# A gated short-convolution layer in split fp32: the products of each piece of weights in other orders

## The chip, the cores and the metric

One core of a Trainium2 chip runs the whole layer in one launch. The metric is device time in microseconds, as the median of several executions.

## The reference

With depth 1 the reference is one layer of 256 tokens and 2048 features, 4096 channels wide:

```python
h = rmsnorm(x, norm_g)
shift, scale, gate = split(silu(c) @ ada_w + ada_b, 3)
h = h * (1 + scale) + shift
b_gate, c_gate, v, g = split(h @ w_in, 4)      # w_in: 2048 x 16384
u = causal_depthwise_conv(c_gate * v, conv_w)  # width 3
y = (b_gate * u * silu(g)) @ w_out             # w_out: 4096 x 2048
x = x + gate * y
return rmsnorm(x, final_g)
```

Everything is float32. The two large products are with `w_in` (134 MB) and `w_out` (33.5 MB); `ada_w` (50 MB) is multiplied by a single vector.

## The kernel before

**Split numbers.** A float32 number is kept as two parts whose sum is the number: `hi`, the number rounded to what one pass of TensorE carries (type float32r), and `lo`, the rest. `split(raw, n)` (lines 187 to 193) makes them from a piece of weights: ACT casts `raw` to `hi` (L191), then DVE subtracts (L192). The tokens lie in `hT` as two such parts, `hh_` and `hl_` (256 columns each, one beside the other), and `y` likewise. A product of two split numbers takes three terms: hi by hi, hi by the tokens' lo, and the weights' lo by hi. The fourth, lo by lo, is left out.

**Start (`mm_s`).** While adaLN's shift and scale are still being summed up from `ada_w` (on DVE, lines L236 and L238), products are already taken for 16 of the 32 channel tiles: four chunks (`ch`) of four tiles (`CT`), each in its four quarters of `w_in`. `plan()` (L41) writes out by hand in which order pieces of `ada_w` are loaded and parts of products are taken. `part(ch, q, k0, k1)` takes the products of feature tiles k0 to k1 for one quarter of a chunk. It loads pieces of up to 2048 numbers per partition, splits them, and for each feature tile and each of the four channel tiles `m` issues three products of 256 columns, one behind another: L286 (hi by `hh_`), L291 (hi by `hl_`), L292 (lo by `hh_`). Two channel tiles share a PSUM bank; `acc` sums up the parts (ACT for the first, DVE L300 for the others). Where adaLN's sums of a group of features are complete, TensorE turns them (`tp_g`, L247), and the tokens of these features get their scale and shift.

**Middle (`mm_b`).** The other 16 channel tiles are taken two at a time, in eight rounds (`ct`), each over the four quarters, each quarter in two pieces of eight feature tiles. For each piece, the loop over `m` (two tiles, a bank each) stands outside and the loop over the feature tile `i` inside; each `i` issues one product of 512 columns (L382: hi by both parts of the tokens) and one of 256 columns (L385: lo by `hh_`). Beside that the gate's columns of `ada_w` are loaded and summed up (`gate_piece`, with its product `ps_gate`, L362).

**End (`mm_o`).** The product with `w_out` runs over four blocks of 512 output columns (`dc`). `out_mm` takes a piece of four channel tiles for one of the two tiles of tokens (`t`) with three products of 512 columns per channel tile: L426 (y hi by hi), L427 (y hi by lo), L428 (y lo by hi). In the last block the last three pieces of the second token tile are held back (`late`), so that the first token tile's norm runs beside them.

**What sets the order.** Every engine works through its own queue in order. All loads are issued by SP. A scheduler orders each queue when the program is built, by its own estimate of times; so the order in the source is where it starts from, not the order that runs. `raw`, `hi` and `lo` have three buffers each, the product banks six. Each product loads its weights anew: there are as many LDWEIGHTS as MATMUL instructions.

Of the kernel before, what the change touches and what calls it, by code (L numbers as in the profile page):

```python
# [13 lines left out]
P = 128  # L14
D = 2048
E = 4096
T = 256
KT = D // P
NCT = E // P
# [10 lines left out]
# In units of the load of one 128 x 128 block: how far adaLN's loads stay behind the products, what lies between the  # L30
# load of a feature tile's columns and its use, and the products of one block.
# [3 lines left out]
# Numbers per partition of a piece of w_in or w_out and of a piece of ada_w; slots of CT * T numbers.  # L35
# [53 lines left out]
def short_conv_layer(ctx: ExitStack, tc: tile.TileContext, x, c, norm_g, ada_w, ada_b, w_in, conv_w, w_out, final_g, out):  # L89
# [49 lines left out]
    # The square root's table is fetched before the squares' sum asks for it.  # L139
# [24 lines left out]
    # The tokens' transpose lies in xs until its features' scale and shift are known, then in hT as two parts that  # L164
    # sum to it.
# [21 lines left out]
    def split(raw, n):  # L187
        """raw = hi + lo, exactly, each of them a number that one pass carries."""
        hi = wpool.tile([P, SLOT], F32R, tag="hi", name="hi", bufs=3)
        lo = wpool.tile([P, SLOT], F32R, tag="lo", name="lo", bufs=3)  # L190
        nc.scalar.copy(hi[:, :n], raw[:, :n])  # L191
        nc.vector.tensor_tensor(out=lo[:, :n], in0=raw[:, :n], in1=hi[:, :n].bitcast(F32), op=ALU.subtract)  # L192
# [23 lines left out]
    def ada_piece(k0, nk, piece):  # L216
# [5 lines left out]
        # Two sums in turn where nothing else stands between them.  # L222
# [20 lines left out]
        # The sum over partitions: turned, then summed along the free axis.  # L243
# [20 lines left out]
    def part(ch, q, k0, k1):  # L264
        """The products of feature tiles k0 to k1 for one quarter of a chunk."""
        col = q * E + ch * CT * P
        step = SLOT // (CT * P)
        banks = [psum.tile([P, 512], F32, tag="mm", name="mm_s") for _ in range(CT // 2)]
        for s0 in range(k0, k1, step):
# [8 lines left out]
            for i in range(sk):  # L278
                k = s0 + i
                hh, hl = hh_[:, k], hl_[:, k]  # L280
                for m in range(CT):
                    o = slice((i * CT + m) * P, (i * CT + m + 1) * P)
                    dst = banks[m // 2][:, (m % 2) * T : (m % 2 + 1) * T]
                    # One start per bank: it clears the whole bank's flags, so the other half's first product lands.
                    opens = k == k0 and m % 2 == 0
                    first = nc.tensor.matmul(dst, hi[:, o], hh, start=opens, stop=False, skip_group_check=True)  # L286
                    if opens:
                        opener = first
                    elif k == k0:
                        tc.add_manual_dep(first.ins, opener.ins.name, after, reason="the bank's flags are cleared first")  # L290
                    nc.tensor.matmul(dst, hi[:, o], hl, start=False, stop=False, skip_group_check=True)  # L291
                    nc.tensor.matmul(dst, lo[:, o], hh, start=False, stop=k == k1 - 1, skip_group_check=True)  # L292
# [11 lines left out]
    def mixed(ch):  # L304
        """y of a chunk's channel tiles, whose four parts are in acc."""
# [61 lines left out]
    for ct in range(NS, NCT, 2):  # L367
        for q in QUARTERS:
            banks = [psum.tile([P, 2, T], F32, tag="mm", name="mm_b") for _ in range(2)]
            col = q * E + ct * P  # L370
            for kp in range(0, KT, KP):
# [6 lines left out]
                for m in range(2):  # L378
                    for i in range(KP):
                        k = kp + i  # L380
                        o = slice((i * 2 + m) * P, (i * 2 + m + 1) * P)
                        nc.tensor.matmul(  # L382
                            banks[m].rearrange("p a t -> p (a t)"), hi[:, o], hT[:, k, :], start=k == 0, stop=False, skip_group_check=True
                        )
                        nc.tensor.matmul(banks[m][:, 0, :], lo[:, o], hh_[:, k], start=False, stop=k == KT - 1, skip_group_check=True)  # L385
# [33 lines left out]
    def out_mm(po, t, ep, hi, lo):  # L419
        for i in range(EP):  # L420
            ct = ep * EP + i
            y = ys[ct // 2][:, ct % 2]
            yh = y[:, 0, t * P : (t + 1) * P]
            yl = y[:, 1, t * P : (t + 1) * P]
            o = slice(i * 512, (i + 1) * 512)
            nc.tensor.matmul(po, yh, hi[:, o], start=ct == 0, stop=False)  # L426
            nc.tensor.matmul(po, yh, lo[:, o], start=False, stop=False)  # L427
# [85 lines left out]
```

## Time and profile before

| | us |
|---|---|
| median of 3 runs | 954.27 |
| lowest, highest | 953.95, 955.4 |
| profiled execution: span from the first to the last instruction | 951.9 |

The profiled execution has no time of its own beside its span; the median lies 2.4 us above that span, and this is taken for what lies around it. Instruction starts are recorded; the ends of matmuls are modelled, so that a matmul is drawn longer than the distance to the next one. The distance between starts is what a product costs.

### The profile page before, as it was taken

To read this page: it belongs to the slowest core of one execution; us is meant where nothing else is said; L and a number is where in the kernel's file an instruction comes from. 1 tells how busy PE (TensorE), PEld (TensorE's weight loads), DVE (VectorE), ACT (ScalarE), POOL (GpSimd) and SP (SyncE) were. 2 spreads that over 40 slices of the span, in tenths; PEclk is the share of its full clock that TensorE was granted. 3 is DMA by queue.
4 is the path that set the end of the run, shared out by engine and by line. 5 is a ranking of instruction groups with operands and counts; after the bars stand their busy time and mean duration, and the time that the engine had idled before them with its cause. 6 is when DMAs were issued, how large, how long until landed. Compare 5 with 4: busy or idle time off the path is not lost.

```text
span 951.9 us, 14329 instructions
## 1 busy us (share of the span) xinstructions
PE 917.5 (96%) x5963; PEld 834.8 (88%) x5963; DVE 667.7 (70%) x785; ACT 418.2 (44%) x468; POOL 0.7 (0%) x6
## 2 busy tenths in 40 slices
PE   3699999999999999999999999999999999999996
PEld 2699999999999999988888888888888878888884
DVE  4798998899899998997565556556555654454533
ACT  6575342443435444444443544444444433433332
POOL 0000000000000000000000000000000000000000
PEclk9799999999999999999999999999999999999998
DMA  9999997999988887886655665565556585665532
GB/s 271 298 360 368 283 337 251 326 329 321 366 296 290 256 261 237 281 298 200 198 195 178 193 203 179 185 199 190 177 184 201 191 309 180 198 198 177 180 130 88
DMA packets 172048, 227.51 MB, mean 239 GB/s; under 512 B 5792, under 2 KB 112464, under 8 KB 171600
## 3 DMA queue, kind: packets, MB, share of 16 engines
q1 hardware_dynamic: 171984, 226.61, 73.0%
q8 instruction: 46, 0.75, 0.3%
q14 instruction: 18, 0.15, 0.0%
HBM read 224.49 MB, written 2.10 MB: 238 GB/s over the span
## 4 chain that ended last, share of the span: by engine, by line
PE 90%; DMA 4%; DVE 3%; issue 1%; ACT 1%; SPq 1%; ACTq 0%; DVEq 0%
PE mm_b L382 25%; PE mm_b L385 13%; PE mm_s L292 11%; PE mm_s L286 11%; PE mm_s L291 11%; PE mm_o L427 6%; PE mm_o L426 6%; PE mm_o L428 6%; DMA raw_s<-in_sc_w_in_dram 2%; DMA at<-in_ada_w_dram 2%; DVE lo L192 1%; DMA x<-in_x_dram 1%; DVE gv L238 1%; ACT hi L191 0%; SPq L231 0%
## 5 line engine op out<-in xcount | busy, mean ns | idle before, releaser
L382 PE MATMUL mm_b<-hT,hi 128*128 128x512 f32 x1024 | 355.2, 392 | 0.0
L286 PE MATMUL mm_s<-hT,hi 128*128 128x256 f32 x1024 | 286.9, 284 | 9.2 <-ACT hT L261 4.9
L291 PE MATMUL mm_s<-hT,hi 128*128 128x256 f32 x1024 | 287.2, 283 | 0.0
L385 PE MATMUL mm_b<-hT,lo 128*128 128x256 f32 x1024 | 285.4, 280 | 0.0
L292 PE MATMUL mm_s<-hT,lo 128*128 128x256 f32 x1024 | 282.9, 283 | 1.4 <-DVE lo L192 1.3
L192 DVE TENSOR_TENSOR lo<-raw,hi 128x2048 fp32r<-128x2048 f32 x64 | 146.6, 2291 | 128.4 <-ACT hi L191 128.3
L382 PEld LDWEIGHTS mm_b<-hT,hi 128*128 128x128 f32 x1024 | 192.1, 188 | 42.3 <-issue 0.2
L191 ACT CAST hi<-raw_s 128x2048 fp32r<-128x2048 f32 (+3 forms) x85 | 126.5, 1489 | 177.5 <-PE mm_s L291 120.7
L286 PEld LDWEIGHTS mm_s<-hT,hi 128*128 128x128 f32 x1024 | 194.3, 191 | 10.2 <-ACT hT L261 5.1
L291 PEld LDWEIGHTS mm_s<-hT,hi 128*128 128x128 f32 x1024 | 195.1, 191 | 0.2 <-issue 0.2
L292 PEld LDWEIGHTS mm_s<-hT,lo 128*128 128x128 f32 x1024 | 191.9, 190 | 2.3 <-DVE lo L192 2.1
L385 PEld LDWEIGHTS mm_b<-hT,lo 128*128 128x128 f32 x1024 | 192.3, 188 | 0.5 <-issue 0.2
L191 ACT CAST hi<-raw 128x2048 fp32r<-128x2048 f32 x64 | 122.4, 1912 | 158.0 <-PE mm_b L382 103.1
L192 DVE TENSOR_TENSOR lo<-raw_s,hi 128x2048 fp32r<-128x2048 f32 (+3 forms) x85 | 149.5, 1759 | 19.7 <-ACT hi L191 19.2
L192 DVE TENSOR_TENSOR lo<-raw_o,hi 128x2048 fp32r<-128x2048 f32 x32 | 73.4, 2292 | 85.4 <-ACT hi L191 85.4
L191 ACT CAST hi<-raw_o 128x2048 fp32r<-128x2048 f32 x32 | 61.2, 1913 | 105.1 <-PE mm_o L428 92.3
L427 PE MATMUL mm_o<-lo,y 128*128 128x512 f32 x256 | 101.8, 399 | 0.0
L426 PE MATMUL mm_o<-hi,y 128*128 128x512 f32 x256 | 101.0, 396 | 0.0
L428 PE MATMUL mm_o<-hi,y 128*128 128x512 f32 x256 | 100.1, 392 | 0.0
L238 DVE SCALAR_TENSOR_TENSOR gv<-at,silu_c,gv 128x512 f32<-128x512 f32 (+1 forms) x149 | 92.2, 639 | 2.6 <-DMA at<-in_ada_w_dram 1.9
L426 PEld LDWEIGHTS mm_o<-hi,y 128*128 128x128 f32 x256 | 48.1, 188 | 12.6 <-issue 0.2
L428 PEld LDWEIGHTS mm_o<-hi,y 128*128 128x128 f32 x256 | 48.1, 188 | 11.5
(80 smaller groups left out, 441.8 us busy)
## 6 DMA issues: line engine op xcount, KB each, us to landing
raw<-in_sc_w_in_dram SPq DMA_DIRECT2D x64, 1024.0 KB, 5.6
raw_s<-in_sc_w_in_dram SPq DMA_DIRECT2D x46, 1024.0 KB, 7.5
at<-in_ada_w_dram SPq DMA_DIRECT2D x128, 256.0 KB, 6.6
raw_o<-in_sc_w_out_dram SPq DMA_DIRECT2D x32, 1024.0 KB, 5.1
at_g<-in_ada_w_dram SPq DMA_DIRECT2D x32, 512.0 KB, 6.8
raw_s<-in_sc_w_in_dram SPq DMA_DIRECT2D x19, 512.0 KB, 5.8
raw_s<-in_sc_w_in_dram SPq DMA_DIRECT2D x7, 768.0 KB, 7.6
raw_s<-in_sc_w_in_dram SPq DMA_DIRECT2D x13, 256.0 KB, 4.5
```

What stands on the lines that cost most here:

```text
L191: nc.scalar.copy(hi[:, :n], raw[:, :n])
L192: nc.vector.tensor_tensor(out=lo[:, :n], in0=raw[:, :n], in1=hi[:, :n].bitcast(F32), op=ALU.subtract)
L238: nc.vector.scalar_tensor_tensor(out=g2, in0=at4[:, i], scalar=c_k, in1=g2, op0=ALU.mult, op1=ALU.add)
L286: first = nc.tensor.matmul(dst, hi[:, o], hh, start=opens, stop=False, skip_group_check=True)
L291: nc.tensor.matmul(dst, hi[:, o], hl, start=False, stop=False, skip_group_check=True)
L292: nc.tensor.matmul(dst, lo[:, o], hh, start=False, stop=k == k1 - 1, skip_group_check=True)
L382: nc.tensor.matmul(banks[m].rearrange("p a t -> p (a t)"), hi[:, o], hT[:, k, :], start=k == 0, stop=False, skip_group_check=True)
L385: nc.tensor.matmul(banks[m][:, 0, :], lo[:, o], hh_[:, k], start=False, stop=k == KT - 1, skip_group_check=True)
L426: nc.tensor.matmul(po, yh, hi[:, o], start=ct == 0, stop=False)
L427: nc.tensor.matmul(po, yh, lo[:, o], start=False, stop=False)
L428: nc.tensor.matmul(po, yl, hi[:, o], start=False, stop=ct == NCT - 1)
```

## The change

The three terms of each piece are issued in other orders. Nothing is added or removed: each product has the same operands and the same bank. In the start the order depends on the chunk, in the middle on the round, at the end on the block. Where a bank's first product must come first, the flag for it and the dependency follow the new order. Comments are dropped too, which moves line numbers only.

```diff
+BIG_ORDERS = [
+    lambda kp: [(i, m, j) for m in range(2) for i in range(kp) for j in range(2)],
+    lambda kp: [(i, m, j) for i in range(kp) for j in range(2) for m in range(2)],
+    lambda kp: [(i, m, j) for m in range(2) for j in range(2) for i in range(kp)],
+    lambda kp: [(i, m, j) for j in range(2) for i in range(kp) for m in range(2)],
+]
+MM_ORDERS = [
+    [(m, j) for m in range(CT) for j in range(3)],
+    [(m, j) for j in range(3) for m in range(CT)],
+    [(m, j) for h in range(2) for j in range(3) for m in (h, h + 2)],
+    [(m, j) for j in range(3) for m in (0, 2, 1, 3)],
+]
...
     def part(ch, q, k0, k1):
...
-            for i in range(sk):
+            terms = [(i, m, j) for i in range(sk) for m, j in MM_ORDERS[ch]]
+            for i, m, j in terms:
                 k = s0 + i
-                hh, hl = hh_[:, k], hl_[:, k]
-                for m in range(CT):
-                    o = slice((i * CT + m) * P, (i * CT + m + 1) * P)
-                    dst = banks[m // 2][:, (m % 2) * T : (m % 2 + 1) * T]
...
-                    first = nc.tensor.matmul(dst, hi[:, o], hh, start=opens, stop=False, skip_group_check=True)
...
-                    nc.tensor.matmul(dst, hi[:, o], hl, start=False, stop=False, skip_group_check=True)
-                    nc.tensor.matmul(dst, lo[:, o], hh, start=False, stop=k == k1 - 1, skip_group_check=True)
+                o = slice((i * CT + m) * P, (i * CT + m + 1) * P)
+                dst = banks[m // 2][:, (m % 2) * T : (m % 2 + 1) * T]
...
+                ins = nc.tensor.matmul(
+                    dst, (lo if j == 2 else hi)[:, o], (hl_ if j == 1 else hh_)[:, k], start=opens, stop=j == 2 and k == k1 - 1, skip_group_check=True
+                )
...
                 hi, lo = split(raw, SLOT)
-                for m in range(2):
-                    for i in range(KP):
-                        k = kp + i
-                        o = slice((i * 2 + m) * P, (i * 2 + m + 1) * P)
+                for i, m, j in BIG_ORDERS[(ct - NS) // 2 % 4](KP):
+                    k = kp + i
+                    o = slice((i * 2 + m) * P, (i * 2 + m + 1) * P)
+                    if j == 0:
                         nc.tensor.matmul(
                             banks[m].rearrange("p a t -> p (a t)"), hi[:, o], hT[:, k, :], start=k == 0, stop=False, skip_group_check=True
                         )
+                    else:
                         nc.tensor.matmul(banks[m][:, 0, :], lo[:, o], hh_[:, k], start=False, stop=k == KT - 1, skip_group_check=True)
...
-    def out_mm(po, t, ep, hi, lo):
+    def out_mm(po, ts, ep, hi, lo, order):
         for i in range(EP):
...
+            if order == 0:
+                terms = [(t, j) for t in ts for j in range(3)]
+            elif order == 1:
+                terms = [(t, j) for j in range(3) for t in ts]
+            else:
+                terms = [(t, j) for t in ts for j in (0, 2, 1)]
...
-            out_mm(po[0], 0, ep, hi, lo)
-            if dc == 3 and ep >= n_ep - LATE:
-                late.append((ep, hi, lo))
-            else:
-                out_mm(po[1], 1, ep, hi, lo)
+            if dc == 3:
+                out_mm(po, [0], ep, hi, lo, 0)
+                if ep >= n_ep - LATE:
+                    late.append((ep, hi, lo))
+                else:
+                    out_mm(po, [1], ep, hi, lo, 0)
+            else:
+                out_mm(po, [0, 1], ep, hi, lo, dc)
```

The first entry of each list is the order of before, so chunk 0, the rounds 0 and 4 of the middle and block 3 of the end keep theirs. In block 0 only the loop over the two token tiles moves inside the loop over the channel tiles.

More of the change, by code (lines that the diff above doesn't have):

```diff
@@ L277, in part @@
             hi, lo = split(raw, n)
[L278 removed]
+            terms = [(i, m, j) for i in range(sk) for m, j in MM_ORDERS[ch]]
+            for i, m, j in terms:
                 k = s0 + i
[L280 to L292 removed]
+                o = slice((i * CT + m) * P, (i * CT + m + 1) * P)
+                dst = banks[m // 2][:, (m % 2) * T : (m % 2 + 1) * T]
+                opens = k == k0 and m % 2 == 0 and j == 0
+                ins = nc.tensor.matmul(
+                    dst, (lo if j == 2 else hi)[:, o], (hl_ if j == 1 else hh_)[:, k], start=opens, stop=j == 2 and k == k1 - 1, skip_group_check=True
+                )
+                if opens:
+                    openers[m // 2] = ins
+                elif k == k0 and j == 0:
+                    tc.add_manual_dep(ins.ins, openers[m // 2].ins.name, after, reason="the bank's flags are cleared first")
         if k0 == 0:
```

13 lines of the change are left out of this document (7 added, 6 removed).

## The prediction

> **What bounds the kernel now.** I read the page's head first, then the table of waits of TensorE, then a table of time stretches inside each stage, and last the order in time at the joints.
>
> ```profile
> span 951.9 us, 14329 instructions
> PE 917.5 (96%) x5963; PEld 834.8 (88%) x5963; DVE 667.7 (70%) x785; ACT 418.2 (44%) x468; POOL 0.7 (0%) x6
> PE 90%; DMA 4%; DVE 3%; issue 1%; ACT 1%; SPq 1%; ACTq 0%; DVEq 0%
> ```
>
> ```profile
> engine line waited for: us in total, times, longest us
> PE tp_x L175 <- ACT x L160: 10.6, 1, 10.6
> PE mm_s L286 <- ACT hT L261: 4.9, 1, 4.9
> PE mm_s L286 <- ACT hi L191: 4.3, 1, 4.3
> PE mm_s L292 <- DVE lo L192: 1.3, 2, 0.8
> ```
>
> TensorE (PE) is busy for 96% of the span and makes up 90% of the chain that ended last. Its waits lie almost all in the first 55 us, before the products can flow, and hang on loads and casts that this change keeps. After that it waits once, for 0.5 us. So the time is the sum of the distances between products, and an order can change the time in two ways only: by changing these distances, or by making TensorE wait for operands.
>
> The distances are read from stretches without a wait. The columns are: stretch, length, then busy time and count of PE and PEld, DVE and so on, the granted clock, the share of the DMA engines.
>
> ```profile
> core 0: us, PE busy (x) PEld busy (x) DVE busy (x) ACT busy (x) POOL busy (x), PEclk, DMA share, GB/s
> 92.00:128.00 36.00, 36.00 (x309) 36.00 (x309) 34.06 (x45) 15.45 (x19) 0.00 (x0) 1.00 0.96 312
> 130.00:165.00 35.00, 35.00 (x294) 35.00 (x293) 31.17 (x44) 11.24 (x14) 0.00 (x0) 1.00 0.84 268
> 270.00:320.00 50.00, 50.00 (x423) 50.00 (x423) 47.97 (x70) 20.76 (x20) 0.00 (x0) 1.00 0.87 291
> 330.00:400.00 70.00, 70.00 (x592) 70.00 (x591) 64.50 (x78) 30.35 (x26) 0.00 (x0) 1.00 0.80 252
> 440.00:660.00 220.00, 220.00 (x1271) 193.69 (x1270) 126.34 (x122) 98.96 (x100) 0.00 (x0) 1.00 0.60 191
> 780.00:920.00 140.00, 140.00 (x601) 112.63 (x600) 69.27 (x47) 51.52 (x37) 0.00 (x0) 1.00 0.57 188
> ```
>
> A stretch counts every product that overlaps it, also the one or two begun before it (a 256-column product is drawn 0.28 us long); two are taken off, one in the last row. The first four rows are the start, all 256 columns wide: 36.00/307 = 117.3 ns, 35.00/292 = 119.9, 50.00/421 = 118.8, 70.00/590 = 118.6. The fifth is the middle, 512 and 256 columns in turn: 220.00/1269 × 2 = 346.7 ns a pair. The last is the end, all 512 wide: 140.00/600 = 233.3 ns. The clock is fully granted (1.00) in all of them.
>
> Two things are to be seen. First, the start has more than one rhythm with the same instructions: 117.3 ns up to 128 us, 119.9 after 130. What stands between them is a set of four turns:
>
> ```profile
> start us, us, engine line op out<-in xcount [idle before <-releaser]
> 128.20 0.28 PE L291 MATMUL mm_s<-hT,hi 128*128 128x256 f32 x1
> 128.32 0.60 PE L247 MATMUL tp_g<-ident,gv 128*128 128x128 f32 x4
> 128.68 0.36 PE L292 MATMUL mm_s<-hT,lo 128*128 128x256 f32 x1
> 128.88 0.28 PE L286 MATMUL mm_s<-hT,hi 128*128 128x256 f32 x1
> ```
>
> From 330 to 400 us no turns intervene and the rhythm stays, over many pieces, banks and weights. So an interruption draws the rhythm, not an operand. Second, a wide and a narrow product in turn cost less than each among its own kind: 233.3 + 118.7 = 352.0 ns against 346.7.
>
> **The change part by part.** Counts, operands, loads and splits stay; what moves is who stands beside whom. I take that from the order of the instructions as built, which carries no times.
>
> *End (`mm_o`).* All 768 products are 512 wide. Their three lines came in a fixed turn, so the 233.3 ns is a mean over neighbours that share y (L426, L427), share the bank, or share neither (at the change of `t`). Blocks 0 to 2 permute these; block 3, and with it the last 192 products and the tail, is as before. I take 0. In blocks 0 to 2 both banks of a block now close together instead of one early; six banks for two in use cover the eviction, and without that cover it would be one bank's eviction by DVE, under 1 us per block.
>
> *Middle (`mm_b`).* Rounds 0 and 4 keep the turn of wide and narrow. Rounds 1 and 5 issue two wide, two narrow; rounds 2 and 6 eight and eight; rounds 3 and 7 sixteen and sixteen. In the built order 593 wide products follow a wide one and 593 narrow ones a narrow one; before it was 5 and 5. So 588 times a step from wide to narrow and one back (346.7 ns together) become one from wide to wide and one from narrow to narrow. With 233.3 from the end and 118.7 from the commonest rhythm of the start, each costs 352.0 − 346.7 = 5.3 ns: 588 × 5.3 = +3.1 us. With the other rhythms of the start (117.3, 119.9) it is 3.9 to 6.5 ns, +2.3 to +3.8 us. The few wide runs of before are shorter than these:
>
> ```profile
> 412.47 0.85 PE L382 MATMUL mm_b<-hT,hi 128*128 128x512 f32 x3
> 413.16 0.28 PE L385 MATMUL mm_b<-hT,lo 128*128 128x256 f32 x1
> ...
> 423.58 1.09 PE L382 MATMUL mm_b<-hT,hi 128*128 128x512 f32 x4
> 424.50 0.28 PE L385 MATMUL mm_b<-hT,lo 128*128 128x256 f32 x1
> ```
>
> Three take 413.16 − 412.47 = 0.69 us and four 0.92: 230 ns each, nothing extra. That sets the lower end: if runs stay at 230, only the narrow neighbours cost, 230 + 118.7 − 346.7 = 2.0 ns, +1.2 us; with a narrow step of 116.7 (346.7 − 230, the step inside a pair) it is 0. I take +3.1, since 464 of the 593 lie in runs of eight and sixteen, nearer to the stretch of 600 than to runs of three; the range keeps 0 to +3.8.
>
> Here a rule stands against the rows. The Trainium skill ("TensorE: Matmul & The Clock Gate", section "Wait — 56ns, not 53.3ns?") gives a warm start-to-start distance of columns/2.4 GHz + 2.5 ns, that is 215.8 and 109.2 ns as estimates by it, whoever stands beside. By that the middle would not change at all, +0 in place of +3.1 us. The trace disagrees on the size (233.3, and 117.3 to 119.9) and on the sum of a pair (346.7, not 352.0).
>
> *Start (`mm_s`).* All 3072 products are 256 wide, so the mix of neighbours can't change. But the turns now cut the stream at other places, and each draws the rhythm anew. A step between neighbouring rhythms is 1.3 ns, 4.0 us if it held for all 3072. The stage as it runs averages about 118.5, so the bounds are 3072 × (117.3 − 118.5) = −3.7 and 3072 × (119.9 − 118.5) = +4.3 us. With some ten draws that partly cancel I take 0, and ±1.3 as the likely spread.
>
> *Operands.* In the middle and at the end the lead of the splits is long: ACT waits for TensorE to free `hi`, not the other way round.
>
> ```profile
> ACT hi L191 <- PE mm_s L291: 126.2, 44, 6.3
> ACT hi L191 <- PE mm_b L382: 105.7, 48, 3.8
> ACT hi L191 <- PE mm_o L428: 92.3, 26, 3.7
> ACT hi L191 <- DMA raw_s<-in_sc_w_in_dram: 28.6, 14, 4.2
> ```
>
> The last row is where it is thin: 14 times in the start the cast waited for its load. The one wait after 55 us comes from there:
>
> ```profile
> 165.39 1.91 ACT L191 CAST hi<-raw_s 128x2048 fp32r<-128x2048 f32 x1 [3.77 <-DMA raw_s<-in_sc_w_in_dram]
> 167.33 2.29 DVE L192 TENSOR_TENSOR lo<-raw_s,hi 128x2048 fp32r<-128x2048 f32 x1 [2.46 <-ACT hi L191]
> 177.05 0.38 PE L292 MATMUL mm_s<-hT,lo 128*128 128x256 f32 x1 [0.53 <-DVE lo L192]
> ```
>
> In the built order of SP, 30 loads of weights move behind one to four loads of `ada_w`, most of them two, and six move ahead; most of the 30 are after the piece used at 180 us. Passing two costs their issue (0.88 us below) and at times their own wait for a buffer (33.7/33 = 1.0 us):
>
> ```profile
> 170.31 0.88 SPq L231 DMA_DIRECT2D at<-in_ada_w_dram  x2
> SPq L231 <- DVE gv L238: 33.7, 33, 2.7
> ```
>
> So a piece lands 1 to 2 us later, and its split with it. Against that, the new orders of chunks 1 and 3 ask for `lo` only after eight products instead of two, which forgives 6 × 118.7 ns = 0.7 us; chunk 2 asks after four. One wait gives all later pieces its length as lead, so waits do not add up piece by piece. I take +0.5 us, bounds −0.5 (the one wait gone) and +4 (two pieces in a row late by 2 us). In the first 50 us the queues of ACT, DVE and SP are as before but for a few neighbours; nothing is counted there.
>
> **Sum.** 951.9 + 0 + 3.1 + 0 + 0.5 = 955.5 us of span; with the 2.4 us that the median (954.27) lies above the span, 957.9.
>
> **The rivals.** *No cost of neighbours* (0.22): the step from wide to wide stays at 230 ns and narrow to narrow falls to 116.7, so the middle keeps 346.7 per pair. For it: the runs of three and four above. Against it: 600 wide products in a row at 233.3, and the narrow stretches, none under 117.3. Span 951.9 + 0.5 = 952.4, time 954.8, give or take the 1.3 of the rhythm. The rule of the Trainium skill quoted above comes out here.
>
> *Late loads* (0.14): weights behind `ada_w` loads reach the cast too late, and TensorE waits for `lo` or `hi` between 165 and 270 us, 3 us more than I count. For it: DMA share 0.84 to 0.96 there, the 14 waits of the cast, the 30 loads set back. Against it: TensorE lost 0.5 us there before, and the new orders ask for `lo` later. Span 958.5, time 960.9.
>
> *The order draws a faster rhythm* (0.08): with the weights, the bank or both changing from each product to the next, narrow products of the start fall into the 116.7 ns that a narrow step has inside a pair. 3072 × (116.7 − 118.5) = −5.5 us; the middle then costs 588 × (233.3 + 116.7 − 346.7) = +1.9. Span 951.9 − 5.5 + 1.9 + 0.5 = 948.8, time 951.2. It decides from a mean of the start below 118.5 − (1.9 + 0.5 + 1.9)/3072 = 117.1 ns. For it: three rhythms exist, so a fourth may. Against it: the same rhythm held from 330 to 400 us across every kind of neighbour in the old order.
>
> That the scheduler undoes the new orders is excluded by the built order: 593 neighbours of a kind against 5.
>
> **How the numbers follow.** The forecast, with the spread of the rhythm, has 0.56. The range 954.2 to 961.5 holds nearly all of it (956 to 960), most of the first rival and the lower part of the second; left out are the faster rhythm (0.08), the lower edge of the first rival and the upper part of the second (0.06 each). About 0.2%, 1.9 us, can be told from no change: below 952.4 or above 956.2. Faster: 0.07 of the third rival and a rest of the first, 0.08. Same: most of the first rival and the low edge of the forecast, 0.26. Slower: the rest, 0.66.
>
> **What would show it.** In the rounds 1 to 3 and 5 to 7 of the middle a pair should take 350.6 to 353.2 ns on average (44.4 us per round before, 45.0 after in the rounds with runs of eight and sixteen), and 346.7 in rounds 0 and 4. The end should keep 233.3 ns in every block. The start should show rhythms from 117.3 to 119.9 that change at the turns only. The waits of PE on `lo` and `hi` after 55 us should stay below 1.5 us. The prediction is wrong if the end changes its distance with the order, if a chunk of the start has a rhythm of its own, or if rounds 1 to 3 keep 346.7.

## The result, and the profile after

| | before | after |
|---|---|---|
| median, us | 954.27 (5 runs, 952.5 to 955.57) | 959.67 (5 runs, 959.0 to 963.87) |
| ratio | | 1.0073 (1.0051 to 1.0094) |
| profiled execution: span, us | 951.9 | 957.9 |

The profiled execution of after took 959.67 us itself. The change made the kernel slower by 0.73%. The stage lengths below come from profiled executions and are compared with each other, since every run with both on record has its span about 1.8 us under its time (959.67 − 957.9 here).

The head of the page after, to be read beside the one before: TensorE is still busy for 96% of the span and carries 90% of the chain that ended last.

```profile
span 957.9 us, 14333 instructions
PE 922.7 (96%) x5963; PEld 836.1 (87%) x5963; DVE 666.3 (70%) x785; ACT 416.4 (43%) x468; POOL 0.7 (0%) x6
PE 90%; DMA 4%; DVE 2%; ACT 1%; issue 1%; SPq 1%; ACTq 0%; DVEq 0%
```

The same 5963 products keep TensorE busy for 922.7 us instead of 917.5: most of the loss lies in the products themselves. Where, is seen by the first product of each stage, in the timeline of TensorE, first of before, then of after (start, duration of the group, engine, line, tile, count). The products of the start are L302 now, those of the middle L398 (wide) and L402 (narrow), those of the end L449.

```profile
27.15 0.79 PE L286 MATMUL mm_s<-hT,hi 128*128 128x256 f32 x2 [4.88 <-ACT hT L261]
...
406.92 0.40 PE L382 MATMUL mm_b<-hT,hi 128*128 128x512 f32 x1
...
763.27 0.80 PE L426 MATMUL mm_o<-hi,y 128*128 128x512 f32 x1
```

```profile
26.82 1.01 PE L302 MATMUL mm_s<-hT,hi 128*128 128x256 f32 x3 [4.90 <-ACT hT L277]
...
408.87 0.39 PE L398 MATMUL mm_b<-hT,hi 128*128 128x512 f32 x1
...
453.96 0.63 PE L398 MATMUL mm_b<-hT,hi 128*128 128x512 f32 x2
...
456.07 0.63 PE L398 MATMUL mm_b<-hT,hi 128*128 128x512 f32 x2
...
498.27 2.04 PE L398 MATMUL mm_b<-hT,hi 128*128 128x512 f32 x8
500.14 1.11 PE L402 MATMUL mm_b<-hT,lo 128*128 128x256 f32 x8
501.09 2.04 PE L398 MATMUL mm_b<-hT,hi 128*128 128x512 f32 x8
502.96 1.11 PE L402 MATMUL mm_b<-hT,lo 128*128 128x256 f32 x8
503.91 0.87 PE L398 MATMUL mm_b<-hT,hi 128*128 128x512 f32 x3
...
543.32 3.91 PE L398 MATMUL mm_b<-hT,hi 128*128 128x512 f32 x16
547.07 2.04 PE L402 MATMUL mm_b<-hT,lo 128*128 128x256 f32 x16
548.95 2.27 PE L398 MATMUL mm_b<-hT,hi 128*128 128x512 f32 x9
...
769.25 0.79 PE L449 MATMUL mm_o<-hi,y 128*128 128x512 f32 x1
```

| us | before | after | difference |
|---|---|---|---|
| to the first `mm_s` | 27.15 | 26.82 | −0.3 |
| start | 379.8 | 382.05 | +2.3 |
| middle | 356.35 | 360.4 | +4.0 |
| end and tail | 188.6 | 188.6 | 0 |

In the middle the rows give the price of a pair by the order that surrounds it. Two wide, two narrow: three such fours, six pairs, from 453.96 to 456.07, 351.7 ns a pair. Eight and eight: 16 pairs from 498.27 to 503.91, 352.5 ns. Sixteen and sixteen: 16 pairs from 543.32 to 548.95, 351.9 ns. In turn (wide, narrow, wide, narrow) it was 346.7. From its first start to its last, each round took 44.26 to 44.30 us before (44.66 in the one that holds the gate's product). After, rounds 0 and 4 take 44.28 and 44.26, rounds 1 and 5 44.89, rounds 2 and 3 44.93 and 45.03, rounds 6 (with the gate's product) and 7 45.20 and 45.05. The three rows above are short and read to 0.01 us; a whole round, its length and one narrow step of 0.12 us by 128 pairs, gives 351.6 ns for the twos of round 1, 352.0 for the eights of round 2 and 352.7 for the sixteens of round 3. The blocks of the end keep 44.57 us each, the first 44.97 beside 44.99.

In the start, the waits of TensorE have changed. First all of them, then stretches of it (length; busy time and count of PE, PEld, DVE and ACT; clock; DMA):

```profile
engine line waited for: us in total, times, longest us
...
PE mm_s L302 <- ACT hT L277: 5.2, 2, 4.9
PE mm_s L302 <- DVE lo L208: 3.6, 3, 2.3
PE mm_s L302 <- ACT hi L207: 3.2, 1, 3.2
```

```profile
60.00:165.00 105.00, 105.00 (x889) 105.00 (x888) 95.06 (x124) 48.70 (x66) 0.00 (x0) 1.00 0.97 321
165.00:200.00 35.00, 31.70 (x267) 31.28 (x266) 30.55 (x38) 11.50 (x15) 0.00 (x0) 1.00 0.93 306
200.00:400.00 200.00, 200.00 (x1678) 199.04 (x1677) 186.64 (x235) 86.83 (x96) 0.00 (x0) 1.00 0.88 290
```

The stretch of 165 to 200 us in before:

```profile
165.00:200.00 35.00, 34.47 (x292) 34.27 (x291) 30.54 (x39) 16.31 (x24) 0.00 (x0) 1.00 0.94 309
```

TensorE stood for 35.00 − 31.70 = 3.3 us between 165 and 200 us, against 0.5, and issued 25 products fewer there. Counted at equal numbers of products, after is 1.4 us ahead at 55 us (an early wait for `hi` of 3.2 us instead of 4.3), 0.9 ahead at 187, 1.6 behind just after that, 1.9 behind at the end of the start, and 6.0 at the end of the middle.

The wait at 187 us, in the timeline of after (SPq is the queue of loads, with the time to issue them; in brackets the idle time before and what ended it):

```profile
170.90 5.67 SPq L290 DMA_DIRECT2D raw_s<-in_sc_w_in_dram  x2
177.54 0.88 SPq L247 DMA_DIRECT2D at<-in_ada_w_dram  x2
...
181.46 1.91 ACT L207 CAST hi<-raw_s 128x2048 fp32r<-128x2048 f32 x1 [5.78 <-PE mm_s L302]
...
184.51 0.49 DVE L252 TENSOR_SCALAR gv<-at,silu_c 128x512 f32<-128x512 f32 x1 [2.94 <-DMA at<-in_ada_w_dram]
184.91 0.74 DVE L254 SCALAR_TENSOR_TENSOR gv<-at,silu_c,gv 128x512 f32<-128x512 f32 x1
185.57 0.68 DVE L316 TENSOR_TENSOR acc<-mm_s,acc 128x512 f32<-128x512 f32 x1
186.18 1.40 DVE L254 SCALAR_TENSOR_TENSOR gv<-at,silu_c,gv 128x512 f32<-128x512 f32 x2
187.50 2.28 DVE L208 TENSOR_TENSOR lo<-raw_s,hi 128x2048 fp32r<-128x2048 f32 x1
...
189.84 0.39 PE L302 MATMUL mm_s<-hT,lo 128*128 128x256 f32 x1 [2.31 <-DVE lo L208]
```

TensorE waits for `lo`, yet its weights were there: the cast that makes `hi` was done at 181.46 + 1.91 = 183.37, and DVE could have subtracted then. But the scheduler has put adaLN's first sum of feature tiles 12 and 13 (L252) ahead of this split in DVE's queue, and that sum waited 2.94 us for its piece of `ada_w`, whose load had been issued at 177.54. The split began 4.1 us after its cast was done; without the wait, the work of DVE that stands ahead of it would have ended 2.94 us earlier. In before, that first sum (L236) stands behind the split:

```profile
180.16 5.27 SPq L231 DMA_DIRECT2D at<-in_ada_w_dram  x6
...
185.04 2.29 DVE L192 TENSOR_TENSOR lo<-raw_s,hi 128x2048 fp32r<-128x2048 f32 x1 [0.52 <-ACT hi L191]
187.25 0.75 DVE L238 SCALAR_TENSOR_TENSOR gv<-at,silu_c,gv 128x512 f32<-128x512 f32 x1
189.48 0.49 DVE L236 TENSOR_SCALAR gv<-at,silu_c 128x512 f32<-128x512 f32 x1 [1.49 <-DMA at<-in_ada_w_dram]
```

There the same piece of `ada_w` (the 97th and 98th issue of `at` in either kernel) is issued later, at 180.16, and waited for too (1.49 us), but no product waits behind it. So the change did not make this load late; it put the sum that needs it ahead of the split. The Trainium skill ("PSUM — Partial Sum Buffer", section "Engine vs sequencer instructions") calls the queues of ScalarE, VectorE and GpSimd strict FIFO. These rows agree: 2.94 us on one load held back a split whose operands were there.

### The profile page after: what moved, and what is told of

Same layout as the page of the kernel before. It is cut to its first block, busy times and chain, and to the rows that moved or that the text cites. A ratio compares the mean times of both kernels' runs of the same rounds, so it can differ in the third digit from the quotient of the medians.

```text
span 957.9 us, 14333 instructions
## 1 busy us (share of the span) xinstructions
PE 922.7 (96%) x5963; PEld 836.1 (87%) x5963; DVE 666.3 (70%) x785; ACT 416.4 (43%) x468; POOL 0.7 (0%) x6
## 4 chain that ended last, share of the span: by engine, by line
PE 90%; DMA 4%; DVE 2%; ACT 1%; issue 1%; SPq 1%; ACTq 0%; DVEq 0%
PE mm_s L302 34%; PE mm_b L398 25%; PE mm_o L449 18%; PE mm_b L402 13%; DMA raw_s<-in_sc_w_in_dram 2%; DMA at<-in_ada_w_dram 2%; DVE lo L208 1%; DVE gv L254 1%; DMA x<-in_x_dram 1%; ACT hi L207 1%; SPq L247 0%; PE ps_gate L378 0%; PE tp_g L263 0%; ACT big L500 0%; DVE big L499 0%
## 5 line engine op out<-in xcount | busy, mean ns | idle before, releaser
L302 PE MATMUL mm_s<-hT,hi 128*128 128x256 f32 x2048 | 318.4, 283 | 8.4 <-ACT hT L277 5.2
L398 PE MATMUL mm_b<-hT,hi 128*128 128x512 f32 x1024 | 297.3, 395 | 0.0
L302 PEld LDWEIGHTS mm_s<-hT,hi 128*128 128x128 f32 x2048 | 281.1, 190 | 9.1 <-ACT hT L277 5.7
L302 PE MATMUL mm_s<-hT,lo 128*128 128x256 f32 x1024 | 205.8, 283 | 3.7 <-DVE lo L208 3.6
L398 PEld LDWEIGHTS mm_b<-hT,hi 128*128 128x128 f32 x1024 | 180.3, 188 | 30.1 <-issue 0.5
L402 PE MATMUL mm_b<-hT,lo 128*128 128x256 f32 x1024 | 190.7, 280 | 0.0
L402 PEld LDWEIGHTS mm_b<-hT,lo 128*128 128x128 f32 x1024 | 163.3, 188 | 16.1
L302 PEld LDWEIGHTS mm_s<-hT,lo 128*128 128x128 f32 x1024 | 158.3, 190 | 5.0 <-DVE lo L208 4.5
L449 PE MATMUL mm_o<-hi,y 128*128 128x512 f32 x512 | 155.8, 396 | 0.0
L449 PEld LDWEIGHTS mm_o<-hi,y 128*128 128x128 f32 x512 | 96.1, 188 | 23.8 <-ACT hi L207 0.2
L449 PE MATMUL mm_o<-lo,y 128*128 128x512 f32 x256 | 95.8, 395 | 0.0
L254 DVE SCALAR_TENSOR_TENSOR gv<-at,silu_c,gv 128x512 f32<-128x512 f32 (+1 forms) x149 | 92.5, 640 | 4.0 <-DMA at<-in_ada_w_dram 3.4
L449 PEld LDWEIGHTS mm_o<-lo,y 128*128 128x128 f32 x256 | 48.1, 188 | 11.7 <-issue 0.2
L316 DVE TENSOR_TENSOR acc<-mm_s,acc 128x512 f32<-128x512 f32 x80 | 51.8, 682 | 3.6 <-PE mm_s L302 3.6
L375 DVE SCALAR_TENSOR_TENSOR gacc<-at_g,silu_c,gacc 128x512 f32<-128x512 f32 x60 | 44.4, 745 | 0.2
```

What stands on the lines that cost most here:

```text
L254: nc.vector.scalar_tensor_tensor(out=g2, in0=at4[:, i], scalar=c_k, in1=g2, op0=ALU.mult, op1=ALU.add)
L302: ins = nc.tensor.matmul(dst, (lo if j == 2 else hi)[:, o], (hl_ if j == 1 else hh_)[:, k], start=opens, stop=j == 2 and k == k1 - 1, skip ...
L316: nc.vector.tensor_tensor(out=a, in0=bank, in1=a, op=ALU.add)
L375: nc.vector.scalar_tensor_tensor(out=ga, in0=at3[:, i, :], scalar=s, in1=ga, op0=ALU.mult, op1=ALU.add)
L398: nc.tensor.matmul(banks[m].rearrange("p a t -> p (a t)"), hi[:, o], hT[:, k, :], start=k == 0, stop=False, skip_group_check=True)
L449: nc.tensor.matmul(po[t], yj, (lo if j == 1 else hi)[:, o], start=ct == 0 and j == 0, stop=ct == NCT - 1 and j == terms[-1][1], skip_group ...
```

## The experiments

### The parts one by one

Three kernels ask which part costs what: the new orders of the middle alone (`mid_only`), of the start alone (`start_only`), and the whole change with the sum held behind the split (`after_pin`).

`mid_only`: against the changed kernel,

```diff
-MM_ORDERS = [
-    [(m, j) for m in range(CT) for j in range(3)],
-    [(m, j) for j in range(3) for m in range(CT)],
...
-]
+MM_ORDERS = [[(m, j) for m in range(CT) for j in range(3)]] * 4
...
-                out_mm(po, [0, 1], ep, hi, lo, dc)
+                out_mm(po, [0], ep, hi, lo, 0)
+                out_mm(po, [1], ep, hi, lo, 0)
```

> The new orders in the middle alone; start and end in their old orders (the start as built is that of before). Theory W (a middle that keeps strict turns of wide and narrow has 346.7 ns a pair, any other mix of the same products about 351.6 to 352.7): the middle, from its first product to the first of the end, takes 360.4 us as with the whole change, against 356.4 before; rounds 0 and 4 keep 44.4 us. Time +4.0 us, ratio 1.0042. Rival S (the middle's cost is handed over by the new start, a phase that it leaves): the middle takes 356.4 us and the time stays within 1 us.

Measured: 957.7 us against 953.71, ratio 1.0046 (1.0034 to 1.0058). The middle took 360.41 us, each round within 0.02 us of its time in the whole change; the start took 379.93. So theory W holds: the orders of the middle alone cost 4.0 us, whatever happens before.

`start_only`: against the changed kernel, the middle in its old order, and the end as above.

```diff
-BIG_ORDERS = [
-    lambda kp: [(i, m, j) for m in range(2) for i in range(kp) for j in range(2)],
-    lambda kp: [(i, m, j) for i in range(kp) for j in range(2) for m in range(2)],
...
-]
+BIG_ORDERS = [lambda kp: [(i, m, j) for m in range(2) for i in range(kp) for j in range(2)]] * 4
```

> The new orders in the start alone (its queues as built are those of the whole change); middle and end in their old orders. Theory W: the middle falls back to 356.4 us. The start, from its first product to the first of the middle, keeps the wait of over 2 us near 187 us and takes 382 us against 379.8 before. Time +2 us, give or take 1.5 for the loads of the first 50 us. Rival S: the middle takes 360.4 us here too, time +6 us. A third theory, that the wait is chance of the loads and not of the queues: no wait over 1 us between 165 and 200 us, time within 1 us.

Measured: 954.95 us (11 runs) against 953.71, ratio 1.0016 (1.0004 to 1.0027), or 1.5 us. The middle is back at 356.31 us. The waits are there again, 1.8 us in all from 60 to 400 us (L297 and L203 are the product and the split in this kernel):

```profile
PE mm_s L297 <- DVE lo L203: 1.8, 2, 1.0
```

The longest is 1.0 us, not the over 2 us near 187 that was expected, and the start took 380.24 us, not 382. So the wait comes back, but its length differs from one execution to the next.

`after_pin`: adaLN's first sum of feature tiles 12 and 13 may not stand ahead of the split issued before it.

```diff
-        nc.vector.tensor_tensor(out=lo[:, :n], in0=raw[:, :n], in1=hi[:, :n].bitcast(F32), op=ALU.subtract)
+        last_split[0] = nc.vector.tensor_tensor(out=lo[:, :n], in0=raw[:, :n], in1=hi[:, :n].bitcast(F32), op=ALU.subtract)
...
-                nc.vector.tensor_scalar_mul(g2, at4[:, i], c_k)
+                opening = nc.vector.tensor_scalar_mul(g2, at4[:, i], c_k)
+                if last_split[0] is not None and k0 == 12:
+                    tc.add_manual_dep(opening.ins, last_split[0].ins.name, after, reason="sums stay behind the split")
```

> The whole change, but adaLN's first sum of features 12 and 13 on DVE is kept behind the split that precedes it in the source; all queues are as in the changed kernel up to there. Theory Q (the wait near 187 us comes from the DVE queue: a split whose operands are there stands behind a sum that waits for its load): the 2.3 us wait of TensorE goes, the start is 2.3 us shorter than with the whole change (379.8 us), the time 2.3 us below that of the whole change, so +3.1 us against before. Rival L (the weights themselves come late, the sum only stands in the same gap): a wait of 1.5 us or more stays there, and the time stays within 0.8 us of the whole change.

Measured: 957.93 us (6 runs), ratio 1.0047 (1.0035 to 1.0059), that is +4.5 us (3.3 to 5.6), more than the +3.1 that was expected. In the profiled execution the start took 379.34 us (379.8 was expected), and TensorE has no wait between 60 and 400 us. DVE's timeline has the split (L210 here) at 183.47, and the sum (L254) behind it; the row of windows below it has TensorE busy all through:

```profile
183.47 2.29 DVE L210 TENSOR_TENSOR lo<-raw_s,hi 128x2048 fp32r<-128x2048 f32 x1
185.67 0.75 DVE L258 SCALAR_TENSOR_TENSOR gv<-at,silu_c,gv 128x512 f32<-128x512 f32 x1
186.34 1.22 DVE L210 TENSOR_TENSOR lo<-raw_s,hi 128x1024 fp32r<-128x1024 f32 x1
187.47 0.48 DVE L254 TENSOR_SCALAR gv<-at,silu_c 128x512 f32<-128x512 f32 x1
```

```profile
165.00:200.00 35.00, 35.00 (x296) 34.87 (x295) 31.96 (x38) 15.63 (x23) 0.00 (x0) 1.00 0.99 337
```

Beside the timeline of after, this shows the cause of that wait, in one execution of each: the place of one sum in DVE's queue. The time of the kernel is then that of `mid_only` (1.0047 beside 1.0046). How much of the 1.0073 the wait was worth, the intervals can't tell.

### Why a pair costs more: the middle

Three kernels change the old middle one property at a time. `mid_banks` exchanges the loops over `m` and `i`, so that the bank changes with each pair while wide and narrow stay in strict turn.

```diff
-                for m in range(2):
-                    for i in range(KP):
+                for i in range(KP):
+                    for m in range(2):
```

> The kernel before with the middle's two inner loops exchanged in all eight rounds: wide and narrow still in strict turns, but the bank (and the half of the weights) changes with every pair instead of once in a piece. Theory W (widths decide): 346.7 ns a pair, the middle 356.4 us as before. Rival B (what costs is the change of bank or weights from product to product): about 351.6 ns a pair as in round 1 of the changed kernel, the middle 361.4 us.

`mid_twos` issues two wide, two narrow in all eight rounds, within one bank.

```diff
-                    for i in range(KP):
+                    for i, j in [(i0 + d, j) for i0 in range(0, KP, 2) for j in range(2) for d in range(2)]:
```

> The kernel before with two wide, two narrow in all eight rounds, the bank changing only once in a piece as before. Theory W: 351.6 ns a pair as in round 1 of the changed kernel, 8 rounds of 128 pairs times 4.9 ns, the middle 361.4 us, time +5.0 us. Rival B (bank): 346.7 ns a pair, the middle 356.4 us, time +0.

The windows of 440 to 640 us, in `mid_banks` and in `mid_twos`:

```profile
440.00:640.00 200.00, 200.00 (x1156) 176.10 (x1155) 115.76 (x109) 87.33 (x90) 0.00 (x0) 1.00 0.59 190
```

```profile
440.00:640.00 200.00, 200.00 (x1134) 174.70 (x1133) 112.88 (x108) 87.84 (x90) 0.00 (x0) 1.00 0.58 188
```

With two products off each count: 200.00/1154 × 2 = 346.6 ns a pair with the banks changing, and 200.00/1132 × 2 = 353.4 with twos. The middle took 356.37 and 362.62 us; the times are 951.09 and 958.14 beside 951.41 for the kernel before on the same chip, one run each. So the bank is not it (theory B falls), and twos alone cost more than the whole change does in its middle: +6.3 us, W's direction and more than it was given. Rounds 1 to 5 ran at 353.3 ns (45.11 us each), and round 7, behind the gate's product in round 6, at the 351.6 that rounds 1 and 5 of the changed kernel have (44.89 us). The same order has two rhythms, and an interruption stands between them.

`mid_lag` keeps the strict turn, but the narrow product takes another feature tile than the wide one beside it, so that no product re-reads the token columns of its neighbour.

```diff
+                        for j, d in ((0, i), (1, (i + 4) % KP)):
+                            k = kp + d
```

> The kernel before; in the middle the narrow product is issued four feature tiles away from the wide one beside it. Widths are still in strict turns, but the narrow product no longer reads token columns that the wide one before it has just read. Theory R (the middle's 346.7 ns a pair comes from reading the same columns twice running, which every new order of the middle breaks, and which the end in turns never had): about 350 to 352 ns a pair, the middle 359.8 to 361.9 us. Theory W (the turn of the widths alone): 346.7 ns, the middle 356.4 us.

Measured: 954.18 us in one run (951.23 for the kernel before beside it); the middle 356.35 us, 346.7 ns a pair:

```profile
440.00:640.00 200.00, 200.00 (x1156) 176.10 (x1155) 116.72 (x115) 89.23 (x90) 0.00 (x0) 1.00 0.59 190
```

The 3.0 us more are not of the middle, which is where the edit is, and single runs of one kernel differ by as much (951.94 to 956.43 over 23 runs of before). Re-reading the same columns (theory R) does not make a turn cheap.

### The same question at the end

If a strict turn of widths saves time, the end could gain by it. `end_turns` cuts one of the three wide products of each channel tile into two of 256 columns and puts them between the others; `end_twos` has the same four products in the order wide, wide, narrow, narrow; `end_reuse` cuts the third product instead of the second, still in turns.

```diff
-            nc.tensor.matmul(po, yh, hi[:, o], start=ct == 0, stop=False)
-            nc.tensor.matmul(po, yh, lo[:, o], start=False, stop=False)
-            nc.tensor.matmul(po, yl, hi[:, o], start=False, stop=ct == NCT - 1)
+            nc.tensor.matmul(po, yh, hi[:, o], start=ct == 0, stop=False, skip_group_check=True)
+            nc.tensor.matmul(po[:, 0:256], yh, lo[:, o1], start=False, stop=ct == NCT - 1, skip_group_check=True)
+            nc.tensor.matmul(po, yl, hi[:, o], start=False, stop=False, skip_group_check=True)
+            nc.tensor.matmul(po[:, 256:512], yh, lo[:, o2], start=False, stop=ct == NCT - 1, skip_group_check=True)
```

Against these four lines, `end_twos` moves the third to the second place:

```diff
-            nc.tensor.matmul(po[:, 0:256], yh, lo[:, o1], start=False, stop=ct == NCT - 1, skip_group_check=True)
             nc.tensor.matmul(po, yl, hi[:, o], start=False, stop=False, skip_group_check=True)
+            nc.tensor.matmul(po[:, 0:256], yh, lo[:, o1], start=False, stop=ct == NCT - 1, skip_group_check=True)
             nc.tensor.matmul(po[:, 256:512], yh, lo[:, o2], start=False, stop=ct == NCT - 1, skip_group_check=True)
```

and `end_reuse` has yl by hi cut in the place of yh by lo:

```diff
-            nc.tensor.matmul(po[:, 0:256], yh, lo[:, o1], start=False, stop=ct == NCT - 1, skip_group_check=True)
-            nc.tensor.matmul(po, yl, hi[:, o], start=False, stop=False, skip_group_check=True)
-            nc.tensor.matmul(po[:, 256:512], yh, lo[:, o2], start=False, stop=ct == NCT - 1, skip_group_check=True)
+            nc.tensor.matmul(po[:, 0:256], yl, hi[:, o1], start=False, stop=ct == NCT - 1, skip_group_check=True)
+            nc.tensor.matmul(po, yh, lo[:, o], start=False, stop=False, skip_group_check=True)
+            nc.tensor.matmul(po[:, 256:512], yl, hi[:, o2], start=False, stop=ct == NCT - 1, skip_group_check=True)
```

> The kernel before, with the second of the end's three 512-column products (y hi by the weights' lo) cut into two of 256 columns, issued in strict turns: wide, narrow, wide, narrow. Theory W: a wide and a narrow one cost 346.7 ns together, so four products take 693.3 ns where three took 700.0; 256 times 6.7 ns, the end 1.7 us shorter, time -1.7 us, ratio 0.9982. Rival F (each product costs by its own width alone, 233.3 and 118.7 ns, and the middle's 346.7 is particular to its operands): 704.0 ns, the end 1.0 us longer.

> The same instructions as with the end's second product cut in halves and issued in turns, but in the order wide, wide, narrow, narrow. Theory W: 703.3 ns for four products (round 1 of the changed kernel: 233.0 + 234.6 + 118.3 + 117.4), the end 0.8 us longer than before. Rival F (each width has its own price, whatever the order): the same length as with the turns.

> The kernel before with the end's third product (y lo by hi) cut in halves instead of the second, in turns wide, narrow, wide, narrow: the first narrow one reads columns that the wide one before it has just read. Theory R: the first pair takes 346.7 ns and the second 350.0, so 696.7 ns for four against 700.0 with the other cut, the end 0.9 us shorter than before. Theory W with a rhythm of the end's own: 700 ns, the end as before.

The stretch of 780 to 920 us in `end_turns`, `end_twos` and `end_reuse`:

```profile
780.00:920.00 140.00, 140.00 (x802) 122.23 (x801) 69.31 (x48) 51.43 (x37) 0.00 (x0) 1.00 0.55 192
```

```profile
780.00:920.00 140.00, 140.00 (x794) 122.07 (x794) 68.20 (x47) 51.27 (x37) 0.00 (x0) 1.00 0.55 188
```

```profile
780.00:920.00 140.00, 140.00 (x803) 122.25 (x802) 69.30 (x48) 51.45 (x37) 0.00 (x0) 1.00 0.57 192
```

In turns a pair takes 140.00/800 × 2 = 350.0 ns, with either cut; in twos 140.00/792 × 2 = 353.5. (The count of a stretch is uncertain by a product at its edges: in `end_reuse` it is one higher, while from the second block on the blocks of both kernels in turns take 44.68 to 44.70 us and those in twos 45.10, which is 3.3 ns a pair more, or 353.3.) From the first product of the end to the last it is 179.52 and 179.50 us in turns and 181.19 in twos, against 179.39 with three wide products. `end_turns` took 953.92 us (12 runs), ratio 1.0003 (0.9993 to 1.0013): neither the gain that W forecast (−1.7 us) nor the loss of the other theory (+1.0). `end_twos` took 957.51 and `end_reuse` 956.43 in one run each; their ends hold +1.8 (+0.8 was expected) and +0.1 us of that, and the rest is a long start (381.41 and 382.00 us), which the edit doesn't touch. So the order matters at the end too, by 1.7 us for the same instructions. But a strict turn does not give 346.7 ns there as it does in the middle, and the cause of that is open. It isn't the re-read operand: the cut of the other product gives the same 350.0.

`end_kick` asks whether 350.0 was one of several rhythms. Between two blocks, one, two or three transposes of the identity are put behind the last product.

```diff
+        if dc:
+            for o in range(dc):
+                turned = nc.tensor.transpose(tk[:, o, :], ident, ident)
+                tc.add_manual_dep(turned.ins, last_mm[0].ins.name, after, reason="between two blocks")
```

> The end in turns (second product cut in halves) with one, two and three turns of the identity between its blocks, so that each block's rhythm is drawn anew. Theory D (350 ns a pair was the rhythm drawn at the end's begin, as the start's rhythms are drawn at its turns): at least one of the three blocks runs at another rhythm than 350.0 ns, 346.7 among them. Theory P (this pattern with these operands has one rhythm): 350.0 ns in all four blocks.

Measured: 953.59 us in one run; the blocks take 45.10, 44.77, 44.80 and 44.78 us, beside 45.10, 44.68, 44.68 and 44.70 without the transposes. The 0.1 us is the first step behind the transposes (0.32 us in place of 0.23); from there on a pair takes 350.0 ns in all four blocks. The pattern of the end comes back to one rhythm (theory P), and here a new draw (D) falls.

### The rhythm of the start

`start_reuse` exchanges the first two of the three products in the start, so that the operand that stays between neighbours is another.

```diff
-                    first = nc.tensor.matmul(dst, hi[:, o], hh, start=opens, stop=False, skip_group_check=True)
+                    first = nc.tensor.matmul(dst, hi[:, o], hl, start=opens, stop=False, skip_group_check=True)
...
-                    nc.tensor.matmul(dst, hi[:, o], hl, start=False, stop=False, skip_group_check=True)
+                    nc.tensor.matmul(dst, hi[:, o], hh, start=False, stop=False, skip_group_check=True)
```

> The kernel before with the start's first two products exchanged (hi by the tokens' lo, then hi by their hi, then lo by their hi), so that two products running read the same token columns. Theory R: a rhythm under 117.3 ns appears in the start. Theory D: the segments between turns have 117.3, 118.7 or 120.0 ns as before, in another draw; the start takes 376 to 382 us like the runs so far.

Measured: 953.84 us in one run, the start 378.58 us, and between the sets of transposes (`tp_g`, the turns of the prediction) only the steps that are known, 117.3 to 120.0 ns. R falls here too. What draws them is better seen in kernels whose start is that of before, instruction for instruction. From 330 to 400 us, without a transpose, before had 118.6 ns. `mid_banks` has

```profile
330.00:400.00 70.00, 70.00 (x599) 70.00 (x598) 64.97 (x77) 31.11 (x29) 0.00 (x0) 1.00 0.80 259
```

70.00/597 = 117.3 ns. The same instructions in the same order run at one step in one execution and at another in the next. The changed kernel itself shows it: from 60 to 165 us, without a wait, 889 products overlapped the stretch in its first profiled execution, and in its second (`after_again`)

```profile
60.00:165.00 105.00, 105.00 (x894) 105.00 (x894) 95.41 (x124) 48.55 (x66) 0.00 (x0) 1.00 0.96 322
```

The nine kernels with this start, before among them, had starts of 376.6 to 382.0 us, 5.4 us apart, and that is about as wide as the times of a kernel scatter (951.94 to 956.43 over 23 runs of before).

### The whole once more

`after_again` is the changed kernel without an edit, to see what comes back.

> The whole change once more, on another occasion. Theory Q with W: the middle takes 360.4 us (+4.0), TensorE waits again near 175 and near 187 us, over 2 us together where the pinned version had none, and the time is the sum of the parts measured alone, 0.46% for the middle and 0.16% for the start: ratio 1.006, above the pinned version's 1.0047. Rival C (the wait near 187 us was chance in the two executions seen so far): no wait over 0.5 us there, ratio 1.004 to 1.005.

Measured: 958.39 us (5 runs) against 953.87, ratio 1.0051 (1.0037 to 1.0065), lower than the expected 1.006, which lies inside the interval. The middle took 360.39 us and the end 179.37 from its first product to its last, as in the first execution to 0.02 us; the start took 379.8, without the loss of the first time, although it waits again. The waits of TensorE from 60 to 400 us:

```profile
PE mm_s L302 <- DVE lo L208: 2.3, 2, 1.4
```

The wait at 187 us is in all three profiled executions with the new start and the sum ahead of the split, at 1.3 to 2.6 us between two products, and in none with the old start. The one near 175 us (1.1 to 1.3 us between products) is no sign of the change: several old starts have it too, up to 1.3 us.

## Why the prediction was right, and where its steps were off

The time, 957.9, lies 0.05% under the median of `after_again` and 0.2% under the first result; direction and place were right, and the size of the change was forecast too small.

**End, 0.** Held: 44.57 us per block in every order, and 0.02 us of difference in the whole stage. Six banks did cover the late closing.

**Middle, +3.1.** It was +4.0, outside its own bounds (0 to +3.8). The step that failed is the price per neighbour of a kind, 588 exchanges at 5.3 ns. By it a round of twos costs 0.34 us more than a round in turn, one of eights 0.59 and one of sixteens 0.64. Measured, the twos cost 0.63 in both rounds, the eights 0.67 and 0.54, the sixteens 0.77 and 0.79. So it was right for the eights, and of the missing 0.9 us about 0.6 lie in the rounds of two and 0.3 in those of sixteen. In the rounds of two only half of the steps are between products of a kind, so the sum gave them 2.65 ns a pair, and they took 4.9, because the steps from wide to narrow grew as well (mean distances between starts, from the trace):

| transition, mean ns | in turn | twos (round 1) | eights (round 2) | sixteens (round 3) |
|---|---|---|---|---|
| wide to wide | | 233.0 | 233.8 | 234.2 |
| wide to narrow | 229.3 | 234.6 | 233.7 | 234.1 |
| narrow to narrow | | 118.3 | 118.2 | 118.4 |
| narrow to wide | 117.3 | 117.4 | 117.5 | 121.3 |

What costs is above all that the strict turn is broken; the length of the runs matters little: 346.7 ns in turn, 351.6 to 352.7 as the mean of a round otherwise (353.3 in most of `mid_twos`). The sign that the prediction named, 350.6 to 353.2 ns a pair in these rounds, was met; its own sum gave less, 588 × 5.3 / 768 = 4.1 ns over 346.7, or 350.8 on average. The lower bound, that runs stay at 230 ns as the runs of three and four in before did, fell: a few products say nothing of a long stretch. With it fell the rival without a cost of neighbours, and the rule of the Trainium skill named there ("TensorE: Matmul & The Clock Gate", section "Wait — 56ns, not 53.3ns?"), by which the middle would have gained or lost nothing; `mid_only` shows 4.0 us for the order alone.

**Start, rhythm 0 ± 1.3.** Within it: +0.4 us from 187 us to the end of the start in the first execution, and from 55 to 187 us nothing beside the longer wait near 175 (1.28 us between two products, 0.81 before). Most segments of that execution ran at 118.7 ns. That the rhythm changes at interruptions held, and no stretch of the start ran under 117.3 ns, so the rival of a faster rhythm fell. Whether it is fixed for a given program the text had not said: it is drawn per execution.

**Operands, +0.5, and less than 1.5 us of waits after 55 us.** The waits were 3.3 and 2.3 us, in `start_only` 1.8, against 0.5 before: 1.3 to 2.8 us more where 0.5 was counted. That is inside the bounds (to +4), and over the limit that was set. The step that failed is the queue: it was argued from SP's, with weights landing late. At 187 us the weights were in time, and the piece of `ada_w` was issued 2.6 us earlier than in before (177.54 beside 180.16). What held the split back was DVE's order, on which the working had nothing. The late-loads rival had the place and about the size, and not the mechanism. What the new start costs in the mean of runs is 1.5 us (0.4 to 2.6, `start_only`).

**From span to time, 2.4 us.** The runs show 1.8 between a run's span and its time; the first profiled execution was 0.6 us faster than the median. The forecast's sum carried that.

So two terms were too small, the middle by 0.9 us and the start by about 1.0 in the mean of runs, and the 0.6 of the last step made up for part of it. That 957.9 comes so near to `after_again` is partly luck: as a difference +3.6 us was forecast, and the runs gave +7.0 us (4.9 to 9.0) in the first result and +4.9 (3.5 to 6.2) in `after_again`, where the kernel before was 0.4 us faster (953.87). In the first execution the sum (955.5 us of span) was 2.4 short: 0.9 in the middle, 2.5 of waits beyond the term and 0.4 of rhythm, less the 1.4 of the early waits, which were counted at nothing.

## What to carry to other kernels

Products are not free to permute when their widths differ: here the same products cost 4.0 us more in other orders. Read the distance between starts over hundreds of products for each order, not the durations, and not a run of three. A new order in the source also moves work in queues that the edit doesn't name, so look in each queue for an instruction that waits for a load ahead of one that the critical engine needs. Where single executions scatter by some microseconds, compare lengths of stages: the middle repeated to 0.02 us in the four kernels with its new orders, while the times of the kernel before scattered by 4.5.

## What the runs showed of the hardware

- The price of a product depends on its neighbours' widths, not on its own width alone: a wide and a narrow one took 346.7 ns in turn in the middle and 350.0 in turn at the end, and in twos 351.6 or 353.3 in the middle and 353.3 at the end. What fixes these values, and why the end has no 346.7, stays open.
- A long row of narrow products has three steps, 117.3, 118.7 and 120.0 ns, drawn anew at interruptions and differing between executions of the same program, at a granted clock of 1.00 in all. The whole start moved by up to 5.4 us with it and the early waits.
- No order beat the kernel before: `end_turns` lies at 1.0003 (0.9993 to 1.0013), and `mid_banks`, in one run, 0.3 us under it with a middle of the same length.
